# A hybrid decoder layer on one core: where the modulation columns are requested, and where four readers of small transfers stand

## The chip, the cores and the metric

One Trainium2 chip, one of its cores. The metric is the device time of one execution in microseconds (us); lower is better. TensorE is PE below (its weight loads PEld), VectorE is DVE, ScalarE is ACT, GpSimd is POOL; the SyncE queue, SP, issues the DMA transfers of this kernel.

## The reference

One layer with 256 tokens of width 2048: a SwiGLU feed-forward at half weight (FFN1), a mixer of two groups of eight heads (forgetting attention, "fox", and a gated delta rule, "gdn"), a second feed-forward (FFN2), and a final norm. Shift, scale and gate of each part come from one matrix-vector product with the condition `c`: nine vectors of 2048, that is nine times 16 columns of 128 in the kernel's layout.

```python
cond = jax.nn.silu(c)
mod = cond @ ada_w[l] + ada_b[l]
sh1, sc1, gt1, sh2, sc2, gt2, sh3, sc3, gt3 = jnp.split(mod, N_MOD, axis=-1)
h = ada_in(x, norm_g[l, 0], sh1, sc1)
x = x + MACARON_W * gt1 * swiglu(h, ffn_w_gate[l, 0], ffn_w_up[l, 0], ffn_w_down[l, 0])
h = ada_in(x, norm_g[l, 1], sh2, sc2)
x = x + gt2 * hybrid_mixer(h, w_in[l], w_out[l], ...)
h = ada_in(x, norm_g[l, 2], sh3, sc3)
x = x + MACARON_W * gt3 * swiglu(h, ffn_w_gate[l, 1], ffn_w_up[l, 1], ffn_w_down[l, 1])
return rmsnorm(x, final_norm)
```

`ada_in` is an RMS norm, scaled by 1 + scale and moved by shift. Everything is float32. In the mixer the forget gates and the delta rule's decays give one row of 256 cumulated logarithms per head and kind. The kernel needs each of these rows on all 128 partitions, and gets it there by writing the rows to DRAM and reading them back with a broadcast.

## The kernel before

**The weight stream.** All weights of the three parts are one stream of 5392 tiles of 128x128 in the order of use, read in 674 blocks of eight tiles (`Stream.next`). For each block SP fetches 512 KB (`wraw`, L125), ACT rounds it to a high part (`whi`, L128), DVE subtracts to get the low part (`wlo`, L140, called the split), and PE multiplies with both. Raw, high and low blocks have four buffers each (the raw ones five from some point on), so the cast of a block waits until PE is through with the block four before.

**Stages by block.** 0 to 111: gate and up products of the first 28 slices of FFN1, 24 matmuls to a block (L573 to L575); 112 to 167: the down projection of these (L493, L494), with a residual update per output column that is two DVE instructions (L517, L518); 168 to 231 and 232 to 263: gate/up and down of the other 16 slices; 264 to 377: the mixer's projections; 378 to 409: the output projection; 410 to 673: FFN2.

**Modulation columns.** Each of the 144 columns is a transfer of 1 MB (`adat`, L261) and a reduce on DVE that multiplies it with the condition and sums along each row (L265, which shows as two instructions, the reduce and a read of its accumulator). `ada_col` issues one transfer behind the newest weight block's transfer and records its reduce. How many are requested per block is the table `RATE`: pairs of a first block and a number of columns for each block from there on, added up in `owed`; at one, a column is requested. `ada_need` asks for those that a consumer needs and that aren't there yet. Until the mixer the reduce is recorded at once, and Tile's scheduler puts it in DVE's order where it expects its data; in the mixer and after it, it is held back until two blocks later (`settle`, `BEHIND`).

**Chains of the mixer.** While the projections run, chains of small work are advanced by a clock that counts 0.35 to a tile (`tick`): a chain is a generator that yields the time until its next part. `decays(half)` makes the decay matrix `Ln` of four heads: a subtraction from the row block (L929, on DVE) and eight exponentials (L932, on ACT). `keys(h)` prepares the keys of a head, `solve(half)` the triangular inverse of four heads, in which `U0` is read back from DRAM (L1015). `decay(h)` (L908, `dec`) and `fox(h)` (L1174, `fm`) are the start of each head's own work. The rows come by `row_of` (`rw`, L897, one head and kind) and `fetch_rows` (`x`, L921, four heads).

**What orders the work.** An engine runs its instructions in the one order that the scheduler wrote. A DVE instruction that waits for a transfer holds up every split that stands behind it. `tc.issue_after(i)` makes the scheduler place an instruction behind instruction `i`; on another engine than that of `i` it orders by time in the scheduler's plan. SP's queue is filled in the same order, so a small read stands behind the block or the column issued ahead of it.

Of the kernel before, what the change touches and what calls it, by code (L numbers as in the profile page):

```python
# [12 lines left out]
AF = mybir.ActivationFunctionType  # L13
# [3 lines left out]
P = 128  # L17
# [15 lines left out]
GR = 24  # L33
NEG = -1e30

RATE = ((0, 0.5), (28, 0.25), (33, 0.5), (49, 0.25), (56, 0.5), (66, 0.2), (112, 0.5), (168, 0.38), (264, 0.0), (284, 0.255), (376, 0.0), (424, 0.16))
N_BIG, N_GDN = 3, 3
N_FIRST = 2
AHEAD = 4
# [54 lines left out]
class Stream:  # L94
# [36 lines left out]
    def next(self, mat, k, n, width=1):  # L131
        i = len(self.order)
        if i % WB == 0:
            nc = self.nc
            b = i // WB
            r, lo = self.first.pop(0) if self.first else self.block(b)
            self.l = lo.tile([P, WB * P], F32R, name="wlo")
            pace = [r_ for r_ in RATE if r_[0] <= b][-1][1]
            with self.behind():
                lo_ = nc.vector.tensor_tensor(self.l, r, self.h.bitcast(F32), ALU.subtract)  # L140
            with self.tc.issue_after(lo_.ins):
                self.settle(b - BEHIND)
            self.owed += 0.0 if self.quiet else pace
            while self.owed >= 1.0:
                self.owed -= 1.0
                self.side()
        for d in range(width):
            self.order.append((mat, k, n, width, d))
        o = (i % WB) * P
        h, l = self.h[:, o : o + width * P], self.l[:, o : o + width * P]  # L150
        return (h, l) if width == 1 else (woven(h), woven(l))
# [3 lines left out]
def layer_kernel(ctx: ExitStack, tc: tile.TileContext, xrow, c, adaw, cols, cst, w, out, order, dbg=None):  # L155
# [600 lines left out]
    def mixer():  # L756
# [146 lines left out]
        def decay(h):  # L903

            gb = rowg.pop(h)
            gbv = gb.rearrange("p (t j) -> p t j", t=2)
            dd = m2p.tile([P, 2, P], F32, name="dec")
            V.tensor_tensor(dd, bc(C("mU")), gbv, ALU.add)  # L908
            for t in range(2):
                A.activation(dd[:, t], dd[:, t], AF.Exp, bias=ng[:, t, h : h + 1])  # L910
            A.activation(gb, gb, AF.Exp)
            return dd, gb
# [10 lines left out]
        def decays(half):  # L923

            hs4 = slice(4 * half, 4 * half + 4)
            yield 5.0
            rv = rowk[half].rearrange("p h (t j) -> p (h t) j", t=2)
            mL = C("mL").unsqueeze(1).to_broadcast([P, 8, P])
            V.tensor_tensor(Ln[:, hs4].rearrange("p h t j -> p (h t) j"), mL, rv, ALU.subtract)  # L929
            for h in range(4 * half, 4 * half + 4):  # L930
                for t in range(2):
                    A.activation(Ln[:, h, t], Ln[:, h, t], AF.Exp, bias=colS[:, t, 1, h : h + 1])  # L932
            yield 1.0
# [42 lines left out]
        def solve(half):  # L976


            hs4, n = slice(4 * half, 4 * half + 4), 2 * NH // 2
            ht = slice(n * half, n * half + n)  # L980
            V.tensor_tensor(rb2[:, :, hs4], nbeg[:, :, hs4], r2[:, :, hs4], ALU.mult)
            rk = rsqrt(ssk[:, :, hs4], [P, 2, 4], "k")
            V.tensor_tensor(rkb[:, :, hs4], rk, colS[:, :, 4, hs4], ALU.mult)
            Lh = Ln[:, hs4].rearrange("p h t j -> p (h t) j")
            yield 4.0
            for b in range(8):
                r = slice(16 * b, 16 * b + 16)
                with tc.issue_after(W.last):
                    nc.sync.dma_start(ld[ht, b].rearrange("n (r c) -> r n c", r=16), Lh[r, :, r])
                if b % 2:  # L990
                    yield 1.4
            yield 3.0
            B = slice(0, 8 * n)
            blk, xt_, pr = (x[B, j] for j in range(4, 7))
            with tc.issue_after(W.last):
                nc.sync.dma_start(blk, ld[ht].rearrange("n b e -> (n b) e"))
            yield 6.0
            G.memset(xt_, 0.0)
            G.memset(xt_[:, 0:256:17], 1.0)
            bv, xv, pv = (t_.rearrange("p (i j) -> p i j", i=16) for t_ in (blk, xt_, pr))  # L1000
            for i in range(1, 16):
                V.tensor_tensor(pv[:, :i, :i], xv[:, :i, :i], bv[:, i, :i].unsqueeze(1).to_broadcast([8 * n, i, i]), ALU.mult)
                V.tensor_reduce(xv[:, :i, i], pv[:, :i, :i], mybir.AxisListType.X, ALU.add)
                if i % 3 == 0:
                    yield 1.2
            yield 8.0
            with tc.issue_after(W.last):
                nc.sync.dma_start(lt[ht].rearrange("n b e -> (n b) e"), xt_)
            yield 3.0
            U = x[:, 7, :P].rearrange("p (n i) -> p n i", n=n)  # L1010
            with tc.issue_after(W.last):
                nc.sync.dma_start(U, lt[ht].rearrange("n b (q i) -> (b q) n i", q=16))
            yield 5.0
            for q in range(2):
                V.tensor_tensor(  # L1015
                    U0[:, hs4].rearrange("p h t (b i) -> p (h t) b i", b=4)[:, 4 * q : 4 * q + 4],
                    U[:, 4 * q : 4 * q + 4].unsqueeze(2).to_broadcast([P, 4, 4, 16]),
                    C("blk").unsqueeze(1).unsqueeze(3).to_broadcast([P, 4, 4, 16]), ALU.mult)
            if half == 0:
                fetch_rows(1)  # L1020
            yield 1.0
# [148 lines left out]
        def fox(h, qk, vt):  # L1170
            cb = rowf.pop(h)
            fm = m1p.tile([P, 384], F32, name="fm")
            for t, o, wd in ((0, 0, P), (1, P, T)):
                A.activation(fm[:, o : o + wd], cb[:, :wd], AF.Identity, bias=colS[:, t, 0, h : h + 1], scale=-1.0)  # L1174
            V.tensor_tensor(fm, fm, C("foxm"), ALU.add)
            yield 1.0
            pl = psf("plog")
            for t, o, wd in ((0, 0, P), (1, P, T)):
                sl = slice(t * P, (t + 1) * P)
                PE.matmul(pl[:, o : o + wd], qk[:, 0, sl], qk[:, 1, :wd], start=True, stop=True)  # L1180
            lg = spare(12)[:, :384]
            mx_ = tiny.tile([P, 2], F32, name="fmx")
            zz = tiny.tile([P, 2], F32, name="fzz")
            for t, o, wd in ((0, 0, P), (1, P, T)):
                V.tensor_tensor_reduce(lg[:, o : o + wd], pl[:, o : o + wd], fm[:, o : o + wd], 1.0, -3.0e38,
                                       ALU.add, ALU.max, mx_[:, t : t + 1])
            V.tensor_scalar(mx_, mx_, -1.0, None, ALU.mult)
            for t, o, wd in ((0, 0, P), (1, P, T)):
                A.activation(lg[:, o : o + wd], lg[:, o : o + wd], AF.Exp, bias=mx_[:, t : t + 1],
                             accum_out=zz[:, t : t + 1])  # L1190
            yield 3.0
            ppt = psf("ppt")
            for b in range(3):
                PE.transpose(ppt[:, b * P : (b + 1) * P], lg[:, b * P : (b + 1) * P], ident)
            pT = spare(14)[:, :384]
            A.copy(pT, ppt[:, :384])
            yield 1.0
            po = psf("pfo")
            vsl = slice((h % 4) * P, (h % 4 + 1) * P)
            PE.matmul(po[:, :P], pT[:, :P], vt[0][:, vsl], start=True, stop=True)  # L1200
            PE.matmul(po[:, P:T], pT[:, P : 2 * P], vt[0][:, vsl], start=True, stop=False)
            PE.matmul(po[:, P:T], pT[:, 2 * P :], vt[1][:, vsl], start=False, stop=True)
            ss = tiny.tile([P, 2], F32, name="fss")
            for t in range(2):
                j1 = tmp.tile([P, P], BF16, name="j1", tag="j1f")
                A.activation(j1, po[:, t * P : (t + 1) * P], AF.Square, accum_out=ss[:, t : t + 1])
            V.scalar_tensor_tensor(zz, zz, EPS, zz, ALU.mult, ALU.mult)
            V.scalar_tensor_tensor(ss, ss, 1.0 / HD, zz, ALU.mult, ALU.add)
            r = rsqrt(ss, [P, 2], "f")
            on = m1p.tile([P, 2, P], F32, name="on")  # L1210
            for t in range(2):
                V.tensor_scalar(on[:, t], po[:, t * P : (t + 1) * P], r[:, t : t + 1], None, ALU.mult)
            yield 5.0
            pf = psf("pft")
            for t in range(2):
                PE.transpose(pf[:, t * P : (t + 1) * P], on[:, t], ident)
            out_split(h, pf[:, :T], L("foxn"))
# [253 lines left out]
```

## Time and profile before

| what | value |
|---|---|
| runs | 1946.34, 1947.27, 1947.93 us; median 1947.27 |
| profiled execution | 1948.17 us, of which the span is 1946.4 us |
| granted PE clock, mean | 0.994 |
| first use of block 112 (FFN1 down) | 344.16 us |
| first use of block 168 | 495.18 us |
| first use of block 264 (mixer) | 757.0 us |
| first use of block 378 (out projection) | 1151.4 us |
| first use of block 410 (FFN2) | 1239.3 us |

Times in the profile are microseconds from the span's start. A row of the timeline is: start, duration, engine, line, operation, output and inputs, shapes, count, and in brackets how long the engine stood idle before it and what ended that. A row of waits is: engine, what waited, for what; then the sum, the number of waits and the longest, in us. A row of the table by stretches is explained where it is shown.

### The profile page before, as it was taken

How to read it: one execution, taken by the hardware profiler on the slowest of the kernel's cores; microseconds unless marked ns; L12 is line 12 of the kernel's file. 1: busy time of each engine (PE TensorE's matmuls, PEld its weight loads, DVE VectorE, ACT ScalarE, POOL GpSimd, SP SyncE). 2: the span in 40 equal slices, each digit the busy share in tenths (PEclk: the TensorE clock that was granted, in tenths of full speed). 3: DMA queues.
4: the chain of work that ended last, by engine and by line, in shares of the span. 5: the costliest groups of instructions: out<-in, count | busy, mean ns of one | idle time of the engine just before them, and what ended most of it. 6: DMA issues, size and time to landing. Idle time of an engine off the chain costs nothing.

```text
span 1946.4 us, 33719 instructions
## 1 busy us (share of the span) xinstructions
PE 1900.8 (98%) x13086; PEld 1773.9 (91%) x13087; DVE 1558.7 (80%) x2414; ACT 1040.3 (53%) x1645; POOL 56.8 (3%) x55
## 2 busy tenths in 40 slices
PE   8999998999999999999999999999999999999998
PEld 7999998888899988899989999999999999999997
DVE  6999977999999997789987988877777666666654
ACT  7444544433444445857657656665554345554553
POOL 0000000000000021000000002000000000000011
PEclk9999999999999999999999999999999999999999
DMA  9998876999998885687667557677777666666663
GB/s 383 346 359 332 309 259 241 393 386 378 353 354 352 341 333 200 219 294 244 221 232 266 171 184 238 210 264 266 263 263 267 229 201 200 204 198 202 201 201 120
DMA packets 129490, 519.58 MB, mean 267 GB/s; under 512 B 18217, under 2 KB 21545, under 8 KB 111153
## 3 DMA queue, kind: packets, MB, share of 16 engines
q1 hardware_dynamic: 129330, 517.42, 74.0%
q8 instruction: 103, 1.69, 0.3%
q14 instruction: 57, 0.47, 0.1%
HBM read 512.89 MB, written 4.47 MB: 266 GB/s over the span
## 4 chain that ended last, share of the span: by engine, by line
PE 75%; DVE 11%; DMA 5%; issue 5%; ACT 3%; SPq 0%; DVEq 0%; ACTq 0%
PE pd L493 14%; PE pg L489 10%; PE pu L489 10%; PE pd L494 7%; PE pu L490 5%; PE pg L490 5%; DVE wlo L140 4%; PE po L493 3%; DMA adat<-in_ada_dram 2%; PE pgu L575 2%; PE pgu L573 2%; PE pgu L574 2%; PE pp L796 2%; PE pp L797 2%; PE pp L798 2%
## 5 line engine op out<-in xcount | busy, mean ns | idle before, releaser
L140 DVE TENSOR_TENSOR wlo<-wraw,whi 128x1024 fp32r<-128x1024 f32 x674 | 821.0, 1225 | 256.1 <-ACT whi L128 254.8
L128 ACT CAST whi<-wraw 128x1024 fp32r<-128x1024 f32 x674 | 698.9, 1046 | 504.4 <-PE pd L493 150.9
L493 PE MATMUL pd<-hid,whi 128*128 128x512 f32 x1408 | 462.0, 382 | 0.0
L494 PE MATMUL pd<-hid,wlo 128*128 128x256 f32 x1408 | 384.7, 273 | 4.8 <-DVE wlo L140 4.8
L265 DVE CUSTOM_DVE_ANT_0 adat<-adat,cs,colt 128x2048 f32<-128x2048 f32 x142 | 334.9, 2359 | 22.6 <-DMA adat<-in_ada_dram 22.6
L489 PE MATMUL pg<-hs,whi 128*128 128x512 f32 x912 | 302.3, 382 | 0.5 <-DVE shc L440 0.5
L489 PE MATMUL pu<-hs,whi 128*128 128x512 f32 x912 | 302.1, 382 | 0.0
L493 PEld LDWEIGHTS pd<-hid,whi 128*128 128x128 f32 x1408 | 266.0, 189 | 36.8
L494 PEld LDWEIGHTS pd<-hid,wlo 128*128 128x128 f32 x1408 | 270.2, 192 | 8.2 <-DVE wlo L140 8.0
L575 PE MATMUL pgu<-hs,wlo 128*128 128x256 f32 x896 | 240.6, 278 | 14.7 <-DVE wlo L140 14.3
L490 PE MATMUL pu<-hs,wlo 128*128 128x256 f32 x912 | 249.1, 273 | 0.0
L490 PE MATMUL pg<-hs,wlo 128*128 128x256 f32 x912 | 249.1, 273 | 0.0
L573 PE MATMUL pgu<-hs,whi 128*128 128x256 f32 x896 | 244.9, 277 | 0.4 <-ACT whi L128 0.3
L574 PE MATMUL pgu<-hs,whi 128*128 128x256 f32 x896 | 244.4, 276 | 0.0
L489 PEld LDWEIGHTS pg<-hs,whi 128*128 128x128 f32 x912 | 172.4, 189 | 24.8 <-ACT shc L439 0.7
L489 PEld LDWEIGHTS pu<-hs,whi 128*128 128x128 f32 x912 | 172.4, 189 | 23.7
L796 PE MATMUL pp<-hs,whi 128*128 128x256 f32 x656 | 188.9, 289 | 1.1 <-ACT hs L380 1.1
L575 PEld LDWEIGHTS pgu<-hs,wlo 128*128 128x128 f32 x896 | 168.4, 193 | 18.4 <-DVE wlo L140 18.3
L797 PE MATMUL pp<-hs,whi 128*128 128x256 f32 x656 | 182.4, 278 | 0.0
L798 PE MATMUL pp<-hs,wlo 128*128 128x256 f32 x656 | 181.9, 277 | 0.0
L490 PEld LDWEIGHTS pu<-hs,wlo 128*128 128x128 f32 x912 | 175.0, 192 | 1.0 <-DVE wlo L140 0.9
L490 PEld LDWEIGHTS pg<-hs,wlo 128*128 128x128 f32 x912 | 175.1, 192 | 0.6
(334 smaller groups left out, 2581.4 us busy)
## 6 DMA issues: line engine op xcount, KB each, us to landing
wraw<-in_w_dram SPq DMA_DIRECT2D x674, 512.0 KB, 4.5
adat<-in_ada_dram SPq DMA_DIRECT2D x142, 1024.0 KB, 7.5
xr<-in_xr_dram SPq DMA_DIRECT2D x4, 512.0 KB, 5.4
adaf<-in_ada_dram SPq DMA_DIRECT2D x4, 512.0 KB, 8.3
xd<-x SPq DMA_DIRECT2D x4, 512.0 KB, 7.4
rw<-rowd SPq DMA_DIRECT2D x16, 128.0 KB, 4.3
x<-xd SPq DMA_DIRECT2D x4, 512.0 KB, 5.3
out_dram<-o SPq DMA_DIRECT2D x8, 256.0 KB, 2.7
```

Of the source, the lines that this page charges most:

```text
L128: self.cast = self.nc.scalar.copy(self.h, r).ins
L140: lo_ = nc.vector.tensor_tensor(self.l, r, self.h.bitcast(F32), ALU.subtract)
L265: V.tensor_tensor_reduce(t, t, cs, 1.0, L("adab", q, 1), ALU.mult, ALU.add, mod[:, q : q + 1])
L489: PE.matmul(ps, wt[0], both, start=(k == 0), stop=False)
L490: PE.matmul(ps[:, T:], wt[1], part(k, HI), start=False, stop=(k == KD - 1))
L493: PE.matmul(ps, wt[0], act.rearrange("p q (a b) -> p q b a", a=2), start=first, stop=False)
L494: PE.matmul(ps[:, :T], wt[1], woven(act[:, 0]), start=False, stop=last)
L573: PE.matmul(o, wh, part(k, HI), start=first and s == 0, stop=False, skip_group_check=skip)
L574: PE.matmul(o, wh, part(k, LO), start=False, stop=False, skip_group_check=skip)
L575: PE.matmul(o, wl, part(k, HI), start=False, stop=last, skip_group_check=skip)
L796: PE.matmul(pp[i][:, :T], wh, hh, start=(k == 0), stop=False)
L797: PE.matmul(pp[i][:, :T], wh, hl, start=False, stop=False)
```

## The change

Two things. First, `RATE`: from block 90 to block 111 no column is requested where one every five blocks was; from 168 it is 0.4 a block instead of 0.38, from 284 0.285 instead of 0.255. Requests by stage, before and now: blocks 66 to 89 4 and 4, 90 to 111 5 and 0, 112 to 167 28 and 28, 168 to 263 34 and 37, 264 to 377 24 and 26, from 410 on 17 and 17. With the requests after 112 the parity moves: 113, 115, 117 and on before, 112, 114, 116 and on now. Second, four readers of small transfers are placed behind the newest block's split (on DVE: `dec`, the subtraction for `Ln`, the two for `U0`) or cast (on ACT: `fm`), and `decays` of the second half yields 10.0 instead of 5.0 before it starts.

```diff
-RATE = ((0, 0.5), (28, 0.25), (33, 0.5), (49, 0.25), (56, 0.5), (66, 0.2), (112, 0.5), (168, 0.38), (264, 0.0), (284, 0.255), (376, 0.0), (424, 0.16))
+RATE = ((0, 0.5), (28, 0.25), (33, 0.5), (49, 0.25), (56, 0.5), (66, 0.2), (90, 0.0), (112, 0.5), (168, 0.4), (264, 0.0), (284, 0.285), (376, 0.0), (424, 0.16))
@@ Stream.next
             with self.tc.issue_after(lo_.ins):
                 self.settle(b - BEHIND)
+            self.split = lo_.ins
@@ decay(h)
-            V.tensor_tensor(dd, bc(C("mU")), gbv, ALU.add)
+            with tc.issue_after(W.split):
+                V.tensor_tensor(dd, bc(C("mU")), gbv, ALU.add)
@@ decays(half)
-            yield 5.0
+            yield 10.0 if half else 5.0
...
-            V.tensor_tensor(Ln[:, hs4].rearrange("p h t j -> p (h t) j"), mL, rv, ALU.subtract)
+            with tc.issue_after(W.split):
+                V.tensor_tensor(Ln[:, hs4].rearrange("p h t j -> p (h t) j"), mL, rv, ALU.subtract)
@@ solve(half)
-                V.tensor_tensor(
-                    U0[:, hs4].rearrange("p h t (b i) -> p (h t) b i", b=4)[:, 4 * q : 4 * q + 4],
+                with tc.issue_after(W.split):
+                    V.tensor_tensor(
+                        U0[:, hs4].rearrange("p h t (b i) -> p (h t) b i", b=4)[:, 4 * q : 4 * q + 4],
...
@@ fox(h, qk, vt)
-                A.activation(fm[:, o : o + wd], cb[:, :wd], AF.Identity, bias=colS[:, t, 0, h : h + 1], scale=-1.0)
+                with tc.issue_after(W.cast):
+                    A.activation(fm[:, o : o + wd], cb[:, :wd], AF.Identity, bias=colS[:, t, 0, h : h + 1], scale=-1.0)
```

How the order moves, at three places. The first is DVE near block 90 in the first feed-forward: `wlo` is a block's split, `adat` a column's reduce, `tg`, `tu` and `hid` finish a slice. Before:

```order
L140 TENSOR_TENSOR wlo_3488<-wraw_3484,whi_3486 128x1024
L265 ISA adat_3590,mod_124<-adat_3590,cs_86,colt_87 128x2048
L265 ISA mod_124 128x1
L591 TENSOR_TENSOR tg_3432<-pgu_3350,acc_394 128x256
L592 TENSOR_TENSOR tu_3433<-pgu_3350,acc_394 128x256
L140 TENSOR_TENSOR wlo_3528<-wraw_3524,whi_3526 128x1024
L524 TENSOR_TENSOR tu_3433<-tu_3433,tg_3432 128x256
L140 TENSOR_TENSOR wlo_3558<-wraw_3554,whi_3556 128x1024
```

The same place now:

```order
L140 TENSOR_TENSOR wlo_3485<-wraw_3481,whi_3483 128x1024
L140 TENSOR_TENSOR wlo_3525<-wraw_3521,whi_3523 128x1024
L592 TENSOR_TENSOR tg_3429<-pgu_3350,acc_394 128x256
L593 TENSOR_TENSOR tu_3430<-pgu_3350,acc_394 128x256
L525 TENSOR_TENSOR tu_3430<-tu_3430,tg_3429 128x256
L140 TENSOR_TENSOR wlo_3555<-wraw_3551,whi_3553 128x1024
```

The reduce of the column requested behind block 90, which stood three splits ahead of the split of its own block, is gone, and a split follows on a split. (Numbers of buffers and lines are off by a few between the two programs.)

The second is DVE shortly before block 112. Before, the reduce of the column requested behind block 110:

```order
L140 TENSOR_TENSOR wlo_4047<-wraw_4043,whi_4045 128x1024
L508 TENSOR_TENSOR hid_3938<-tu_3933,hid_3938 128x256
L265 ISA adat_4169,mod_124<-adat_4169,cs_86,colt_87 128x2048
L265 ISA mod_124 128x1
L591 TENSOR_TENSOR tg_3981<-pgu_3941,acc_586 128x256
L592 TENSOR_TENSOR tu_3982<-pgu_3941,acc_586 128x256
L140 TENSOR_TENSOR wlo_4087<-wraw_4083,whi_4085 128x1024
```

Now the first reduce after the pause, that of the column requested behind block 112:

```order
L140 TENSOR_TENSOR wlo_4115<-wraw_4111,whi_4113 128x1024
L525 TENSOR_TENSOR tu_3970<-tu_3970,tg_3969 128x256
L592 TENSOR_TENSOR tg_4015<-pgu_3978,acc_595 128x256
L593 TENSOR_TENSOR tu_4016<-pgu_3978,acc_595 128x256
L509 TENSOR_TENSOR hid_3975<-tu_3970,hid_3975 128x256
L266 ISA adat_4237,mod_124<-adat_4237,cs_86,colt_87 128x2048
L266 ISA mod_124 128x1
L525 TENSOR_TENSOR tu_4016<-tu_4016,tg_4015 128x256
L592 TENSOR_TENSOR tg_4061<-pgu_4024,acc_604 128x256
L593 TENSOR_TENSOR tu_4062<-pgu_4024,acc_604 128x256
L140 TENSOR_TENSOR wlo_4155<-wraw_4151,whi_4153 128x1024
```

It too stands three splits ahead of its own block's, behind the split of block 109. In the down projection behind it the fifteen pairs of residual reads (L517 and L518 before, one line further down now) stand where they stood, but for four that have one more split ahead of the pair or between its two reads, and two that have one less.

The third is ACT in the mixer, at block 284: `kk` are keys, `pk` a PSUM bank of theirs, `fm` the fox rows, `Ln` the decays. Before:

```order
L128 CAST whi_9146<-wraw_9144 128x1024
L949 ACTIVATE kk_8972<-cv_8974 128x256
L1074 ACTIVATE kbd_9974<-kk_8611,colS_8276 128x128
L1174 ACTIVATE fm_9640<-rw_9087,colS_8276 128x128
L1174 ACTIVATE fm_9640<-rw_9087,colS_8276 128x256
L945 COPY cp_9077<-pp_8981 128x256
L967 ACTIVATE j1_9065,ssk_8280<-pk_9059 128x128
L932 ACT_TABLE_LOAD
L932 ACTIVATE Ln_8284<-Ln_8284,colS_8276 128x128 x8
L967 ACTIVATE j1_9067,ssk_8280<-pk_9059 128x128
L968 COPY kk_8620<-pk_9059 128x256
```

Now:

```order
L128 CAST whi_9140<-wraw_9138 128x1024
L1078 ACTIVATE kbd_9951<-kk_8605,colS_8270 128x128
L935 ACT_TABLE_LOAD
L935 ACTIVATE Ln_8278<-Ln_8278,colS_8270 128x128 x8
L952 ACT_TABLE_LOAD
L952 ACTIVATE kk_8966<-cv_8968 128x256
L970 ACTIVATE j1_9059,ssk_8274<-pk_9053 128x128
L970 ACTIVATE j1_9061,ssk_8274<-pk_9053 128x128
L971 COPY kk_8614<-pk_9053 128x256
```

The two activations for `fm` are gone from here (they stand behind the cast of block 302 now), and the exponentials stand ahead of the keys' own activations, with a second table load behind them. SP's read for `Ln` stands behind block 285 instead of 284, with no column between. On PE the order is the same but for the keys of heads 4 to 7, which come 14 tiles later, and a few instructions that move by one to three tiles.

More of the change, by code (lines that the diff above doesn't have):

```diff
@@ L1014, in solve @@
             for q in range(2):
-                V.tensor_tensor(
-                    U0[:, hs4].rearrange("p h t (b i) -> p (h t) b i", b=4)[:, 4 * q : 4 * q + 4],
-                    U[:, 4 * q : 4 * q + 4].unsqueeze(2).to_broadcast([P, 4, 4, 16]),
-                    C("blk").unsqueeze(1).unsqueeze(3).to_broadcast([P, 4, 4, 16]), ALU.mult)
+                with tc.issue_after(W.split):
+                    V.tensor_tensor(
+                        U0[:, hs4].rearrange("p h t (b i) -> p (h t) b i", b=4)[:, 4 * q : 4 * q + 4],
+                        U[:, 4 * q : 4 * q + 4].unsqueeze(2).to_broadcast([P, 4, 4, 16]),
+                        C("blk").unsqueeze(1).unsqueeze(3).to_broadcast([P, 4, 4, 16]), ALU.mult)
             if half == 0:
```

## The prediction

> **What bounds the kernel now.** I read the page's busy shares first, then a table by stretches of the program, then the waits and the timeline of the stretch that stands out.
>
> ```profile
> span 1946.4 us, 33719 instructions
> PE 1900.8 (98%) x13086; PEld 1773.9 (91%) x13087; DVE 1558.7 (80%) x2414; ACT 1040.3 (53%) x1645; POOL 56.8 (3%) x55
> ...
> 200.00:260.00 60.00, 60.00 (x540) 60.00 (x539) 54.56 (x81) 32.10 (x45) 0.00 (x0) 1.00 0.82 300
> 265.00:345.00 80.00, 71.36 (x612) 70.25 (x611) 63.23 (x103) 37.56 (x58) 0.00 (x0) 0.98 0.67 237
> 345.00:495.00 150.00, 147.69 (x893) 134.05 (x892) 141.10 (x162) 60.13 (x60) 0.00 (x0) 1.00 0.98 386
> 495.00:660.00 165.00, 164.96 (x1003) 150.76 (x1002) 150.94 (x175) 81.34 (x122) 0.00 (x0) 1.00 0.92 354
> 830.00:1165.00 335.00, 327.38 (x2528) 311.43 (x2527) 289.05 (x710) 219.16 (x477) 0.43 (x2) 1.00 0.66 230
> ```
>
> PE is the bound: 1900.8 of 1946.4 us. What a change of order can win is the rest, 45.6 us, and the stretches (start:end, length, then PE, PEld, DVE, ACT, POOL busy with counts, PE clock, DMA share, GB/s) tell where it lies. From 200 to 260 PE never stops. From 265 to 345, the same stage with the same matmuls, it idles 80 - 71.36 = 8.64 us, though DVE and the DMA engines do less there (63.23 of 80, 0.67) than in the full stretch (54.56 of 60, 0.82). So it isn't for lack of an engine; something stands in a wrong order. At the pace of the full stretch (60 us for 540 matmuls, 0.111 us each, 24 to a block, so 2.67 us a block) the 612 matmuls need 68.0 us: the stretch has lost up to 12.0 us.
>
> ```profile
> PE pgu L575 <- DVE wlo L140: 7.1, 4, 2.8
> PE pd L494 <- DVE wlo L140: 1.5, 1, 1.5
> ...
> 259.03 1.23 DVE L140 TENSOR_TENSOR wlo<-wraw,whi 128x1024 fp32r<-128x1024 f32 x1 [0.52 <-ACT whi L128]
> 263.14 2.35 DVE L265 CUSTOM_DVE_ANT_0 adat<-adat,cs,colt 128x2048 f32<-128x2048 f32 x1 [2.88 <-DMA adat<-in_ada_dram]
> ...
> 270.72 0.43 SPq L261 DMA_DIRECT2D adat<-in_ada_dram  x1
> ...
> 273.90 1.23 DVE L140 TENSOR_TENSOR wlo<-wraw,whi 128x1024 fp32r<-128x1024 f32 x1 [0.52 <-ACT whi L128]
> 278.99 2.35 DVE L265 CUSTOM_DVE_ANT_0 adat<-adat,cs,colt 128x2048 f32<-128x2048 f32 x1 [3.87 <-DMA adat<-in_ada_dram]
> 281.94 1.22 DVE L140 TENSOR_TENSOR wlo<-wraw,whi 128x1024 fp32r<-128x1024 f32 x1
> 283.21 0.38 PE L575 MATMUL pgu<-hs,wlo 128*128 128x256 f32 x1 [1.29 <-DVE wlo L140]
> ...
> 298.94 0.38 PE L575 MATMUL pgu<-hs,wlo 128*128 128x256 f32 x1 [2.07 <-DVE wlo L140]
> 331.64 0.38 PE L575 MATMUL pgu<-hs,wlo 128*128 128x256 f32 x1 [2.78 <-DVE wlo L140]
> ```
>
> All of PE's 8.6 us (7.1 + 1.5, five waits) are for a weight split. The timeline shows why: the split at 273.90 is done at 275.1; the next instruction on DVE is the reduce of a modulation column whose 1 MB was only requested at 270.72 and is there at 279.0. DVE stands for 3.87 us, reduces for 2.35, and only then come the splits behind it: PE runs out and waits 1.29 us. Once every five blocks this repeats. The first column of the row, with 2.88 us of waiting at 263.14, costs PE nothing, so PE has a cushion of about that size, and the ones that follow eat it.
>
> **The change, part by part.** The sum is made against the profiled execution: 1948.17 us, span 1946.4 and 1.8 around it, 0.9 above the median of the runs.
>
> *Term 1, blocks 90 to 112.* Five requests (behind blocks 90, 95, 100, 105, 110) go, and with them the five reduces that stood three splits ahead of their own block. Beside the waits there is a stretch at a lower clock, straight behind the wait of 2.07 us:
>
> ```profile
> 299.00:303.00 4.00, 4.00 (x21) 4.00 (x22) 4.00 (x7) 2.77 (x4) 0.00 (x0) 0.57 0.65 190
> ```
>
> 21 matmuls in 4 us where 36 fit: 15 x 0.111 = 1.7 us lost. With the idle 8.6 that is 10.3 us at least, 12.0 at most by the matmul count above; I take 11.0. Against it stands one column requested in a bunch, behind block 112: its reduce still stands three splits ahead of its own block. It can cost nothing (the cushion is full by then, as at 263.14) or as much as the worst wait here with a slow stretch behind it, 2.78 + 1.7 = 4.5. I take nothing, since it is the first after 27 blocks without one; the ends are -12.0 and -6.5.
>
> *Term 2, the down projection after it (345 to 495).* Both versions request 28 columns there, one every other block, so the work stays; what moves is which blocks get one, and so whether a residual read stands ahead of a split.
>
> ```profile
> PE pd L494 <- DVE wlo L140: 2.3, 7, 0.6
> DVE x L517 <- PE pd L494: 8.0, 7, 2.4
> ```
>
> PE's seven waits (2.3 us, all of that stretch's idle 2.31) and DVE's seven (8.0 us, in a residual read that waits for PE's last product) are as many. In the changed order four of the fifteen pairs of reads stand a split later, so that DVE has one split more done when it waits, and two stand a split earlier; the other nine keep their place. The most to win is 2.3; the other way the waits could double, +2.3. Of eleven parts that stay or get worse against four that get better I make little: -0.5.
>
> *Term 3, the first keys of the mixer.* SP sends two small reads of DRAM behind a 1 MB column; their readers on DVE and ACT stand ahead of other work.
>
> ```profile
> 800.95 1.14 SPq L261 DMA_DIRECT2D adat<-in_ada_dram  x1
> 802.14 0.43 SPq L921 DMA_DIRECT2D x<-rowd  x1
> 802.61 1.26 SPq L897 DMA_DIRECT2D rw<-rowd  x2
> ...
> 810.34 1.22 DVE L929 TENSOR_TENSOR Ln<-cstt,x 128x1024 f32<-128x1024 f32 x1
> 812.58 0.80 ACT L1174 ACTIVATE fm<-rw,colS 128x128 f32<-128x128 f32 x2 [2.80 <-DMA rw<-rowd]
> 813.92 1.28 ACT L932 ACT_TABLE_LOAD   x1
> 815.22 2.44 ACT L932 ACTIVATE Ln<-Ln,colS 128x128 f32<-128x128 f32 x8
> 817.82 0.35 ACT L968 COPY kk<-pk 128x256 f32<-128x256 f32 x1
> 816.35 0.44 PE L961 MATMUL pk<-colt,kk 128*128 128x128 f32 x2 [1.13 <-DVE Ln L974]
> 818.22 1.22 PE L964 MATMUL pkk<-kk 128*128 128x128 f32 x4 [1.22 <-ACT kk L968]
> ...
> 818.00:822.00 4.00, 3.78 (x12) 3.27 (x13) 3.83 (x13) 3.98 (x10) 0.00 (x0) 0.57 0.12 49
> ```
>
> ACT waits 2.80 us for the fox rows; behind that on its queue stand the table load, the eight exponentials (2.44) and the copy that PE waits for: PE loses 1.13 + 1.22, and a clock of 0.57 follows, priced at 1.7 as above: 4.05 in all. The pin on the fox reader puts it some eighteen blocks later, out of this place; the exponentials keep theirs. The read for Ln goes a block later, with no 1 MB column ahead of it; on ACT one more table load (1.28) stands here. The gain lies between 0 (the Ln subtraction waits for its own read instead) and 4.05; I take -3.0, since the 2.80 us that go are more than the 2.35 that PE waits.
>
> *Term 4, the rest of the mixer.* Twenty readers are pinned in all (eight decays, eight fox rows, two Ln, two U0), each behind the newest block's split or cast.
>
> ```profile
> PE pft L1216 <- issue: 1.6, 1, 1.6
> PE po L1130 <- DVE vz L1128: 1.5, 4, 0.7
> PE pvq L1042 <- ACT qv L949: 1.0, 2, 0.6
> PE pfo L1200 <- ACT x L1196: 0.9, 2, 0.5
> ```
>
> PE idles 335 - 327.38 = 7.6 us from 830 to 1165, in small waits on chains of its own, 0.7 us at the longest of those on DVE and ACT. None of these rows names a small read, so little is to be had: at best the two waits of the first fox head (1.6 and 0.9) and a part of the rest, -4. A pinned reader comes later, and who uses its result may be late: 20 x 0.3, under half of the longest wait, is +6. What uses the results keeps its place two or more blocks behind, over 5 us at 2.67 us a block, so I take -1.0.
>
> *Term 5, the columns moved back.* Five go to later stages: three from block 168 to 263, two into the mixer. Each is one reduce of 2.35 us and one transfer. They cost nothing where DVE has room under PE: 150.94 of 165 us busy from 495 to 660, 289.05 of 335 in the mixer. Without that cover it is 5 x 2.35 = 11.8.
>
> Sum: -11.0 - 0.5 - 3.0 - 1.0 + 0 = **-15.5**: 1932.7 for the profiled execution, 1931.8 for a median, 0.8% faster.
>
> **The rivals.**
>
> *R1, the columns in a bunch take a part back.* The request behind block 112 waits like the worst now (4.5), and the down stage gets worse by 2.3 where I took 0.5 off: 1932.7 + 4.5 + 2.8 - 0.9 = 1939.1. For it: the reduce there still stands ahead of its own block. Against: the first such wait cost nothing.
>
> *R2, the pins are late, slower than before.* Behind the newest split a reader waits for a cast and thus for PE; if its chain has no slack, PE waits for each. At 0.7 us, the longest such wait, 20 readers cost 14.0; two slow stretches more 3.4, and terms 3 and 4 don't come: 1936.7 + 17.4 - 0.9 = 1953.2. It decides from 0.6 us a reader (20 x 0.6 is 12.0, and 1936.7 + 11.5 is the profiled execution). Against it: the users stand two blocks behind.
>
> *R3, the slow stretches stay.* Their 2 x 1.7 stay lost if the waits don't cause them: 1932.7 + 3.4 - 0.9 = 1935.2. For it: no such stretch follows the longest wait, 2.78 us, so waiting alone doesn't make one. Against: both lie right behind waits.
> [...]
>
> *R4, the loss only moves.* If the cover of term 5 is gone, 11.8 come back, and 2.8 from the down stage as in R1: 1932.7 + 14.6 - 0.9 = 1946.4, no change. For it: DVE is 94% busy from 345 to 495 (141.10 of 150). Against: none of the five columns goes there.
>
> **How the numbers follow.** The forecast has 0.64, R1 0.13, R3 0.07, R2 0.09, R4 0.07. 0.2% (3.9 us) is about what a measurement of this kernel can tell from no change. Faster by more are the forecast, R1 and R3, 0.84; R4 is same, 0.07; R2 slower, 0.09. The predicted time is the forecast's, 1931.8. The low end takes term 1 at -12.0, term 2 at -2.3, term 3 at -4.05 and half of term 4's best: 1948.17 - 20.4 - 0.9 = 1926.9, and 1926 in round figures; the high end holds R1, 1940. R2 and R4, 0.16, are left out.
>
> **What would show it.** Right: from 265 to 345 PE idles under 1 us and does those 612 matmuls in some 68 us; no column reduce waits for its transfer there; no stretch at 0.57 near 299. In the down stage PE's waits on the split sum to 1 to 2 us. At the first keys ACT doesn't wait for the fox rows, and PE's waits on `kk` and Ln are under 1 us. Wrong: a wait over 2 us behind the reduce of block 112's column; PE waits on `dec`, `fm`, Ln or U0's users in many heads (R2); a clock below 1 with no wait ahead of it (R3); splits late between 495 and 660, where now PE has 164.96 of 165 (R4).

## The result, and the profile after

The changed kernel takes 1939.2 us (median of 6 runs, 1937.09 to 1939.99) against 1947.6 for the kernel before beside it: a ratio of 0.9952, 95% interval 0.994 to 0.9963, or 8.4 us. 1931.8 was forecast, with a range from 1926 to 1940. The profiled execution has a span of 1937.3 us, 9.1 less than before.

First the page's first part and the table by stretches of the changed kernel (start:end, length, then PE, PEld, DVE, ACT, POOL busy with counts, PE clock, DMA share, GB/s):

```profile
span 1937.3 us, 33703 instructions
PE 1897.9 (98%) x13086; PEld 1772.2 (91%) x13087; DVE 1558.3 (80%) x2414; ACT 1038.4 (54%) x1645; POOL 55.6 (3%) x55
```

```profile
265.00:345.00 80.00, 80.00 (x683) 79.00 (x682) 66.12 (x106) 43.24 (x64) 0.00 (x0) 1.00 0.71 248
345.00:495.00 150.00, 147.90 (x895) 134.39 (x894) 140.07 (x161) 57.41 (x58) 0.00 (x0) 1.00 0.98 385
495.00:660.00 165.00, 164.89 (x997) 150.03 (x996) 152.51 (x176) 82.58 (x123) 0.00 (x0) 1.00 0.95 357
818.00:822.00 4.00, 4.00 (x21) 3.49 (x20) 3.41 (x10) 1.06 (x1) 0.00 (x0) 1.00 0.23 29
830.00:1165.00 335.00, 323.38 (x2520) 308.89 (x2519) 290.26 (x711) 219.56 (x481) 0.43 (x2) 0.99 0.65 235
```

PE no longer idles between 265 and 345 (80.00 of 80, where 71.36 stood), and no stretch at 0.57 is left near 299 or 818. But from 830 to 1165 it idles 335 - 323.38 = 11.6 us, where 7.6 stood before: the mixer got worse.

Counting PE's matmuls with the low part gives the time of each block's first use. The lead of a stage is how much earlier its first block starts than in the profile before; a term is the difference of two leads.

| from block to block | lead at the end | this stretch | forecast |
|---|---|---|---|
| 87 to 112 (end of the first gate/up) | 11.5 | -11.5 | -11.0 |
| 112 to 168 (down) | 12.1 | -0.6 | -0.5 |
| 168 to 264 (second gate/up, down) | 9.8 | +2.4 | 0 |
| 264 to 284 (first keys) | 13.8 | -4.1 | -3.0 |
| 284 to 378 (rest of the mixer) | 9.0 | +4.8 | -1.0 |
| 378 to the end | 9.1 | -0.1 | 0 |

The two losses have their rows. The waits of PE, from 655 to 740 (one row) and in the mixer (the four longest kinds):

```profile
PE pd L495 <- DVE wlo L140: 2.0, 4, 0.7
```

```profile
PE po L1134 <- DVE vz L1132: 2.5, 1, 2.5
PE ppt L1199 <- ACT x L1194: 1.5, 1, 1.5
PE po L1131 <- DVE st L1142: 1.3, 3, 0.6
PE pn L1083 <- DVE rsa_o L297: 1.2, 1, 1.2
```

In the down projection before the mixer PE waits four times for a split, 2.0 us; before it was 0.9. In the mixer one wait of 2.5 us for `vz` is new. The timeline of the changed kernel around it, SP, DVE and PE, and then the stretch behind it:

```profile
894.52 3.69 SPq L992 DMA_DIRECT2D ld<-Ln  x8
898.26 0.43 SPq L898 DMA_DIRECT2D rw<-rowd  x1
899.45 0.47 SPq L999 DMA_DIRECT2D x<-ld  x1
899.97 0.59 SPq L262 DMA_DIRECT2D adat<-in_ada_dram  x1
```

```profile
906.36 0.15 DVE L1005 TENSOR_TENSOR x<-x 64x1 f32<-64x1 f32 x1 [2.56 <-DMA x<-ld]
907.60 0.28 DVE L1132 TENSOR_TENSOR vz<-u,po 64x128 f32<-64x128 f32 x1
907.93 0.80 PE L1134 MATMUL po<-vz,At 128*128 128x128 f32 x2 [2.51 <-DVE vz L1132]
```

```profile
908.00:912.00 4.00, 4.00 (x23) 4.00 (x24) 4.00 (x5) 2.88 (x9) 0.00 (x0) 0.63 0.35 120
```

`solve(1)` writes its blocks to `ld` at 894.5 and reads them back at 899.5, just ahead of a column; the read has landed at 906.3, 6.8 us after its issue. The reader, L1005, isn't one of the four that were pinned. DVE stands 2.56 us for it, `vz` is behind it, PE idles 2.51 us and runs the next 3.4 us at a lower clock (0.50 from 907.54 to 910.95).

### The profile page after: what moved, and what is told of

Its sections match the earlier page's. It is cut to its first block, busy times and chain, and to the rows that moved or that the text cites. A ratio compares the mean times of both kernels' runs of the same rounds, so it can differ in the third digit from the quotient of the medians.

```text
span 1937.3 us, 33703 instructions
## 1 busy us (share of the span) xinstructions
PE 1897.9 (98%) x13086; PEld 1772.2 (91%) x13087; DVE 1558.3 (80%) x2414; ACT 1038.4 (54%) x1645; POOL 55.6 (3%) x55
## 4 chain that ended last, share of the span: by engine, by line
PE 77%; DVE 12%; ACT 4%; issue 3%; DMA 2%; SPq 0%; DVEq 0%; ACTq 0%
PE pd L494 13%; PE pg L490 10%; PE pu L490 10%; PE pd L495 7%; PE pu L491 5%; PE pg L491 5%; DVE wlo L140 5%; PE pgu L576 4%; PE pgu L575 4%; PE pgu L574 4%; PE po L494 3%; DVE adat L266 3%; PE pp L797 2%; PE pp L798 2%; PE pp L799 1%
## 5 line engine op out<-in xcount | busy, mean ns | idle before, releaser
L576 PEld LDWEIGHTS pgu<-hs,wlo 128*128 128x128 f32 x896 | 167.8, 192 | 10.5 <-DVE wlo L140 10.4
```

The lines of the kernel that those rows point to most:

```text
L576: PE.matmul(o, wl, part(k, HI), start=False, stop=last, skip_group_check=skip)
```

## The experiments

All are compared with the kernel before on the same chip, in at least five executions each; ratios have their 95% intervals, and a gain in us is worked out from the ratio where nothing else is said. The profiled executions differ by up to 2.5 us before block 20, and by up to 1.6 in the wait at 106, behind which some have a slow stretch of the clock and some have none (the pause alone 0.90 from 100 to 108 and 0.89 from 108 to 116, the kernel before and the changed kernel 1.00 in both); so leads are counted from block 87.

**The pause alone.**

```diff
-... (66, 0.2), (112, 0.5), (168, 0.38), (264, 0.0), (284, 0.255), ...
+... (66, 0.2), (90, 0.0), (112, 0.5), (168, 0.38), (264, 0.0), (284, 0.255), ...
```

> The kernel before with one edit of the table: no columns from block 90 to 111, every later rate as before (0.38 and 0.255), no pins. Theory (the five columns of that stretch cost 11.5 us by their place, and what they do later costs little): block 112 starts 11.5 us earlier, PE has no wait on a split from 265 to 333, the time is about 1947.4 - 11.5 - 0.6 = 1935. Rival (the columns have to be read at some time, and their price comes back further on, where they are forced together): block 112 starts 11.5 us earlier too, but the time is 1943 or more.

Ratio 0.9978 (0.9969 to 0.9988): 4.3 us, the rival. Block 112 leads by 11.5 us, and blocks 168 to 264 lose nothing (12.1 and 12.1). But the lead falls to 8.4 at block 378 and to 4.5 at block 410: the five columns that nobody asked for earlier are forced behind blocks 401 to 409, where the next part needs them. The waits of PE from 1142 to 1245, the output projection:

```profile
PE po L494 <- DVE wlo L140: 2.1, 3, 0.8
PE pg L434 <- DVE wlo L140: 0.8, 1, 0.8
```

In the changed kernel no wait for a split stands there. So about 4 us of the pause's gain hang on the higher rates later.

**The old columns, in another place on DVE.** For the nine columns requested behind blocks 66 to 111, the reduce is held behind the split of its own block; all columns stay where they are requested.

```diff
+            self.split, self.at = lo_.ins, b
...
-            with nullcontext() if W.late else W.behind(False):
+            here = 66 <= len(W.order) // WB < 112
+            with nullcontext() if W.late else tc.issue_after(W.split) if here else W.behind(False):
```

> The kernel before with all its columns at their old blocks, but from block 66 to 111 each reduce is placed behind the split of its own block, not up to three splits ahead of it. Theory (the place of the reduce on DVE is at fault, not its 2.35 us or its 1 MB): PE's waits between 265 and 345 go, block 112 starts 10 us or more earlier, the time is about 1937. Rival (the 1 MB transfer or the 2.35 us of DVE is what PE waits for): the waits stay, the time stays at 1947.

Ratio 0.995 (0.9937 to 0.9962): 9.8 us, as much as the whole change. (Its profile is of the longest of its six runs, 1943.37 against a median of 1939.42, and has a lead of 6.6 at the end.) Block 112 leads by 11.5 us, as with the pause. The stretch, PE's one wait in it, and one of the reduces:

```profile
265.00:345.00 80.00, 79.42 (x683) 78.35 (x682) 72.30 (x112) 43.64 (x66) 0.00 (x0) 1.00 0.81 283
```

```profile
PE pd L496 <- DVE wlo L140: 0.6, 1, 0.6
```

```profile
281.80 1.23 DVE L140 TENSOR_TENSOR wlo<-wraw,whi 128x1024 fp32r<-128x1024 f32 x1 [0.82 <-ACT whi L128]
282.94 2.35 DVE L267 CUSTOM_DVE_ANT_0 adat<-adat,cs,colt 128x2048 f32<-128x2048 f32 x1
```

PE does the same 683 matmuls as in the changed kernel, with DVE at 72.3 us instead of 66.1 and the DMA share at 0.81 instead of 0.71. The reduce no longer waits: its data is there when its own block's split is done. So in this stretch the column's 2.35 us and its 1 MB weren't the trouble.

**The pins alone**, with the later second half of the decays and the old table.

> The changed kernel with the old table of rates: the four pins and the later second half of the decays alone. Theory (pins win 4 us at the first keys, and pins with the later second half lose 4 to 5 us between blocks 300 and 340, where DVE now waits for a read of ld): block 112 starts as before, block 284 is 4 us ahead of before, block 340 about level, the time is 1947 within 1.5. Rival (the loss between 300 and 340 comes from the more frequent columns of the new table): block 340 stays 4 us ahead and the time is 1943 to 1944.

Ratio 0.9982 (0.9972 to 0.9991): 3.5 us, the rival's time; the lead at block 340 lies between the two. Leads: 4.8 at block 284, of which 1.1 are from before block 112 and 3.7 from the first keys; 2.6 at block 340, 3.8 at block 378. The first keys came out as said; the loss behind them is 2.1 up to block 340 and 1.0 up to 378, not 4 to 5. So the loss in the changed kernel isn't the pins' alone.

**The new table alone**, no pins, and both halves of the decays at 5.0.

> The kernel before with the whole new table of rates and no pins. Theory (the pause saves 11.5 us, and the higher later rates are what keeps the five columns from being forced in the output projection, where the pause alone lost 4 us): block 410 stays at the lead of block 378, the time is 8 us below before; with the pins, worth 3.5 alone, the two then overlap. Rival (the higher rates win nothing against the pause alone): 4 to 5 us below before.

Ratio 0.9951 (0.9939 to 0.9963): 9.6 us, all that the whole change has. As said, block 410 stays at the lead of block 378 (9.0 and 9.1). At the first keys it wins 2.1 us, about half of the changed kernel's 4.1, though a wait for the key copy remains. The pause alone wins 1.7 there, with neither a pin nor the new rate of the mixer. Neither profile has the slow stretch that stood near 818 before (0.50 from 818.22 to 821.63), priced at 1.7 in the prediction: the granted clock is 1.00 from 807 to 819 in both, and in the version without the pin on `fm`. From 284 to 378 it loses 2.8. PE's row at the keys and DVE's wait for `ld`:

```profile
809.26 0.60 PE L964 MATMUL pkk<-kk 128*128 128x128 f32 x3 [1.95 <-ACT kk L968]
```

```profile
DVE x L1002 <- DMA x<-ld: 5.3, 1, 5.3
```

This is the first half's read, sent at 825.6 with a column 0.6 us behind it. The pause alone has the same wait, 4.4 us, at the old rate of the mixer, so a late read of `ld` needs neither pins nor denser columns. The second half's read, the one that costs the changed kernel its 2.5 us, is in time here and in the pins alone: DVE doesn't wait for it in either. It is late only where the later half and the new table meet.

**The second half of the decays at 5.0 again**, all else as changed.

```diff
-            yield 10.0 if half else 5.0
+            yield 5.0
```

> The changed kernel with the second half of the decays yielding 5.0 as before, not 10.0. Theory (the later second half is what brings the read of ld behind a column and in front of vz): the wait of 2.5 us at vz near 908 goes, the time is 2 to 4 us below the changed kernel, 12 us below before. Rival (the half that comes earlier meets other readers): the wait goes and others come between blocks 300 and 320, the time is that of the changed kernel, 9 us below before, or more.

Ratio 0.9937 (0.9925 to 0.9949): 12.3 us, the theory. In the profile the lead is 13.9 at block 284 and 13.7 at block 378: of 4.8 us of loss 0.2 is left. The mixer's stretch, and SP and DVE at the read:

```profile
830.00:1165.00 335.00, 327.48 (x2548) 311.97 (x2547) 294.14 (x719) 222.13 (x486) 0.55 (x3) 1.00 0.67 239
```

```profile
894.30 0.48 SPq L999 DMA_DIRECT2D x<-ld  x1
...
897.05 0.42 SPq L262 DMA_DIRECT2D adat<-in_ada_dram  x1
```

```profile
899.59 0.15 DVE L1005 TENSOR_TENSOR x<-x 64x1 f32<-64x1 f32 x1
```

The read goes 2.75 us ahead of the next column instead of 0.5, is there when its reader starts, 5.3 us after the issue (in the changed kernel it takes 6.8), and DVE doesn't wait for it at all. In the changed kernel a column is sent 0.52 us behind this read and DVE waits 2.6 us for it; it waits 2.3 us in that kernel's second profile and 2.9 without the pin on `fm`. The interval overlaps that of the changed kernel (0.994 to 0.9963) by a little; the profile's 4.6 us tell them apart.

**A fifth pin**, on the reader of `ld`.

```diff
-                V.tensor_tensor(pv[:, :i, :i], xv[:, :i, :i], ...)
+                with nullcontext() if i > 1 else tc.issue_after(W.split):
+                    V.tensor_tensor(pv[:, :i, :i], xv[:, :i, :i], ...)
```

> The changed kernel with a fifth reader pinned: the first DVE instruction that reads the 16x16 blocks back from ld stands behind the newest split too. Theory (at 905 DVE stands 2.6 us for that read with vz behind it, PE idles 2.5 us for vz and runs 3.4 us at half clock, which costs another 1.7): both go, the time is 1939.2 - 4.2 = 1935. Rival (the wait goes on to the next link of that chain, U0 or the heads' own solves come late): the wait at vz goes, others of its size come between blocks 320 and 360, the time is 1938 to 1941.

Ratio 0.9946 (0.9934 to 0.9958): 10.5 us, between the two numbers, and by the runs not clear of the changed kernel. DVE's rows:

```profile
908.48 0.28 DVE L1133 TENSOR_TENSOR vz<-u,po 64x128 f32<-64x128 f32 x1
...
916.06 0.14 DVE L1006 TENSOR_TENSOR x<-x 64x1 f32<-64x1 f32 x1
```

`vz` now runs ahead of the reader, which waits for nothing, and PE's wait is gone. The lead at block 320 is 12.6 (9.4 in the changed kernel), at the end 12.1 (9.1): 3.0 us in the profile. No later link of the chain took a wait of that size over: the longest wait of PE behind it is 1.1 us.

**Without the pin on `fm`.**

```diff
-                with tc.issue_after(W.cast):
+                if True:
                     A.activation(fm[:, o : o + wd], ...)
```

> The changed kernel without the pin on fm (ACT); the pins on dec, Ln and U0 stay. Theory (at block 284 the fox reader on ACT held up the exponentials and the key copy, 4 us with the slow stretch): the wait of ACT for the fox rows near 812 comes back, PE waits 1 to 2 us at the first keys, block 300 loses 3 to 4 us of its lead, the time is 6 to 7 us below before. Rival (the later half of the decays and the pin on Ln made that gain): block 300 keeps its lead, the time stays at 9 us below before.

Ratio 0.9962 (0.995 to 0.9974): 7.4 us, not clear of the changed kernel by the runs. In the profile ACT waits 1.0 us for the fox rows again, PE 1.4 for the key copy where 0.3 stood, and the first keys win 3.0 instead of 4.1 us. The pin on `fm` is worth about 1 us there, not the 3 to 4 that the theory gave it; of the rest, 1.7 to 2.1 us come without any pin, as the pause and the table alone show.

**0.38 from block 168**, with the missing columns in the mixer (0.318) and the decays at 5.0.

> The changed kernel with the second half of the decays at 5.0, 0.38 instead of 0.4 from block 168, and 0.318 instead of 0.285 from 284, so that the columns still are there in time. Theory (0.4 is what lost 2.4 us between blocks 168 and 264, the later half of the decays what lost 4 to 5 between 300 and 340): blocks 168 to 264 lose nothing, 13 to 15 us below before. Rival (the three columns that now go into the mixer cost there what they cost before it): blocks 168 to 264 lose nothing, the mixer loses 2 to 3 more, 11 to 12 us below before.

Ratio 0.9955 (0.9942 to 0.9967): 8.8 us, the rival's side, and less than its 11 to 12. Blocks 168 to 264 lose nothing (12.1 and 12.1), so it is the 0.4 that costs 2.4 us; whether by the number of columns or by the blocks that they fall on wasn't tried. The mixer loses 5.7 from block 284 on:

```profile
PE pd L495 <- DVE wlo L140: 0.6, 1, 0.6
```

```profile
858.56 0.38 PE L797 MATMUL pp<-hs,whi 128*128 128x256 f32 x1 [2.29 <-ACT whi L128]
```

One wait is left between 655 and 740 (first row), and the mixer has a new one of 2.29 us for a cast.

**All columns at their old rates, placed, with the pins.** The old table, reduces behind their own blocks' splits from block 66 to the mixer, the pin on `ld`, the second half of the decays at 10.0.

> The changed kernel with the old table of rates, each reduce from block 66 to the mixer placed behind the split of its own block, and the reader of ld pinned. Theory (place is what counts, and the gains add up: 9.8 us of the place alone, 3.5 of the pins alone, 2 to 3 of the ld reader): 13 to 16 us below before. Rival (the later columns of the old table leave a wait in the feed-forward behind the mixer and in its middle): 10 to 12 us below before.

Ratio 0.9936 (0.9924 to 0.9949): 12.5 us, between the two. The lead is 13.5 us at block 498 and 11.1 at block 542. DVE and PE at the start of FFN2's first down projection:

```profile
1466.84 2.35 DVE L267 CUSTOM_DVE_ANT_0 adat<-adat,cs,colt 128x2048 f32<-128x2048 f32 x1 [2.71 <-DMA adat<-in_ada_dram]
...
1472.06 0.42 DVE L510 TENSOR_TENSOR hid<-tu,hid 128x256 fp32r<-128x256 f32 x1
```

```profile
1472.53 0.48 PE L495 MATMUL pd<-hid,whi 128*128 128x512 f32 x1 [2.30 <-DVE hid L510]
```

It is the trouble of blocks 90 to 112 again: the column requested behind block 503 stands three splits ahead of its own block, and `hid` behind it. The same wait, of 2.0 and 1.4 us, is in the profiles of the placed reduces alone and of the pins alone, which have the old table too. The kernel before has the same order and DVE waits only 0.21 us there; why the column comes later in the three wasn't tried.

**The same with 0.2 a block from 424**, so that nothing is requested behind 503.

> The version with the old table, reduces behind their own blocks' splits and the ld reader pinned, with one number more changed: 0.2 instead of 0.16 columns a block from block 424, so that no column is requested behind blocks 503 and 509. Theory (there DVE stood 2.4 to 2.7 us for such a column with the second feed-forward's hid behind it, and PE idled 2.3 us at the start of the last down projection): that wait goes, block 542 keeps the lead of block 498, 13.5 us in the profile, the time is 13 to 15 us below before. Rival (the more frequent columns make another stretch of that stage late): the lead at block 630 is 11 us again.

Ratio 0.9942 (0.9928 to 0.9956), 11.1 us by the medians, 1936.2 (1935.74 to 1939.49). The wait is gone and the lead of block 498, 13.0, is kept to the end (13.1), as the theory has it. The time is short of the 13 to 15 us expected, and by the runs it isn't told apart from the one above.

**A version put together, and the changed kernel again on its chip.** The pins, the placed reduces, both halves of the decays at 5.0, 0.5 from block 111, 0.38 from 168, 0.285 from 284, 0.16 from 429.

> A version put together from the runs so far: the pins with both halves of the decays at 5.0; from block 66 to the mixer each reduce behind the split of its own block, so no pause at 90 but requests at even blocks from 112; 0.38 from 168, 0.285 from 284, 0.16 from 429. Theory (each part keeps what it won alone): 11.5 to 12 us at block 168, no loss from 168 to 264 as with 0.38 before, 3 to 4 at the first keys, nothing lost later: 14 to 16 us below before, 5 to 7 below the changed kernel. Rival (the gains overlap in the mixer): 12 us below before, as with the second half at 5.0 alone.

> The changed kernel once more, on the chip of the version put together: 9 us below before, as in its first comparison (ratio 0.9952); it is what the two others of this call are compared with.

The version takes 1937.89 us (1937.09 to 1938.52), ratio 0.9945 (0.9932 to 0.9957); the changed kernel 1941.49 (1940.70 to 1942.13), 0.9963 (0.995 to 0.9977). On one chip the runs don't overlap: 3.6 us less than the changed kernel, under the 5 to 7 expected; 10.7 below before is also under the rival's 12. It loses 1.8 us from block 112 to 168, where the changed kernel wins 0.6; PE waits there for two splits, 0.96 and 0.45 us, that it doesn't wait for in the changed kernel. The changed kernel's second profile has the same leads as its first, within 0.3 us at each stage and 9.1 at the end.

## Why the prediction was right, and what was mis-sized

The time lies in the range, and the sign and the first two terms came as worked out. That it lies in the range is in part luck: 1939.2 is 7.4 us above the forecast, and the range reached up to 1940 for R1, which didn't happen. The mechanism of term 1 is shown from both sides: take the columns away, or leave them and move only their reduces, and block 112 starts 11.5 us earlier in either case. The column requested behind block 112 cost nothing, as taken. The changed kernel's reduces between 265 and 345 waited 0.2 us in all, and PE has no wait there:

```profile
L266 DVE CUSTOM_DVE_ANT_0 adat<-adat,cs,colt 128x2048 f32<-128x2048 f32 x3 | 7.0, 2339 | 0.2 <-DMA adat<-in_ada_dram 0.2
```

Term 2 was -0.6 against -0.5. Term 3 was -4.1 against -3.0, the full 4.05 that the rows bounded; its cause was told too narrowly, since the pin on `fm` holds only about 1 us of it, and about half came without any pin.

The step that was mis-sized is term 4: "None of these rows names a small read, so little is to be had", with -1.0 and an upper end of +6 for the pinned readers. It cost +4.8, inside the bounds, but not by the pinned readers being late. The rows of before have no wait of PE on a small read in the mixer, but DVE did wait for such reads there, without a wait of PE of that size behind it:

```profile
DVE dec L908 <- DMA rw<-rowd: 2.7, 1, 2.7
DVE U L1015 <- DMA x<-lt: 2.1, 1, 2.1
```

So PE's rows alone didn't tell what a DVE wait of this size would cost with `vz` behind it. The change moved `solve(1)` by the 14 tiles of the later half, and with the new table its read of `ld` left 0.5 us ahead of a 1 MB column. An unpinned reader became the wait. The later half at 5.0 takes 4.6 of the 4.8 back, the fifth pin 3.0.

Term 5 was taken at nothing, for DVE's 14 us of room from 495 to 660; it cost 2.4 (0.4 against 0.38, shown by the version that goes back to 0.38). The stretch that was read for the cover is the gate/up stage, and it loses 0.7 us by the leads, with no wait long enough to name. The other 1.6 are lost in the down projection behind it, where residual reads and columns stand together: two more waits for a split, 2.0 us against 0.9.

R1 gave 1939.1, what was measured, but not by its mechanism: neither the column behind block 112 nor the down stage behind it took anything back. R2 fell: PE has no such wait in many heads. R4 fell for this table, but the pause alone shows how near it was: there the lead shrinks by 5.4 us in the mixer (by which of its waits wasn't tried) and by 3.9 in the output projection, where columns are forced. R3's question is below.

## What to carry to other kernels

In this kernel a wait on a transfer held up what stood behind it on the engine's queue (at 278.99 in the kernel before DVE waits 3.87 us for a column, and PE then 1.29 us for the split behind it), so first ask whether the waiting instruction can stand later, before the transfer is moved or dropped: placing nine reduces behind their own blocks' splits won as much as the whole change. A table of rates is a sum that has to come out: what is left out in one stage is forced in another, and the price there has to be read from that other stage's own rows, down projection and gate/up apart. Whoever moves a chain in time moves its transfers past other transfers (the read of `ld` took 6.8 us with a column 0.52 us behind it, and no more than 5.3 with one 2.75 us behind it); list every reader of DRAM on that chain, pinned or not.

## What was not expected of the hardware

In these profiles the lower clock behind a wait of PE comes or doesn't, at one length of the wait. In the kernel before the wait of 2.07 us had a slow stretch (0.50 from 299.40 to 302.81) and that of 2.78 had none (1.00 from 330.11 to 336.93). The pins alone have waits in the first feed-forward of 2.10 us, with full speed behind it (1.00 from 286 to 290), and of 2.70 us, with a slow stretch (0.64 from 333 to 337). The changed kernel's second profile has a wait of 2.25 us for `vz` and full speed behind it (1.00 from 910 to 914), where the first had a slow stretch behind 2.51 (0.50 from 907.54 to 910.95). So here the length alone doesn't decide.

What goes with it is where the wait falls. In the profiles of the kernel before and of the changed kernel each slow stretch is 3.41 us long or twice that (753.37 to 760.20 and 743.70 to 750.53, but for the one that the end cuts off), and within a profile they all begin on one raster of 3.41 us: in the kernel before, 299.40 and 818.22 are 152 steps apart, in the changed kernel 743.70 and 907.54 are 48. The rows cut the time on that raster. First the kernel before, around its two longest waits (they end at 298.94 and 331.64), then the two profiles of the changed kernel around `vz`:

```profile
295.98:299.40 3.42, 1.35 (x12) 1.16 (x12) 3.42 (x7) 0.56 (x2) 0.00 (x0) 1.00 0.08 31
299.40:302.81 3.41, 3.41 (x19) 3.41 (x18) 3.40 (x6) 2.63 (x4) 0.00 (x0) 0.50 0.71 205
326.70:330.11 3.41, 2.16 (x20) 1.97 (x18) 2.68 (x4) 0.00 (x0) 0.00 (x0) 1.00 0.26 99
330.11:333.52 3.41, 1.88 (x16) 1.88 (x17) 3.41 (x8) 1.98 (x4) 0.00 (x0) 1.00 0.27 64
```

```profile
904.13:907.54 3.41, 1.29 (x12) 1.10 (x10) 1.18 (x12) 2.12 (x6) 0.00 (x0) 1.00 0.87 346
907.54:910.95 3.41, 3.02 (x14) 3.02 (x15) 3.35 (x7) 2.15 (x8) 0.00 (x0) 0.50 0.16 42
```

```profile
905.25:908.66 3.41, 2.44 (x22) 2.25 (x21) 1.03 (x8) 3.26 (x8) 0.00 (x0) 1.00 1.01 403
908.66:912.08 3.42, 2.14 (x19) 2.14 (x20) 3.36 (x16) 1.57 (x7) 0.00 (x0) 1.00 0.13 54
```

The wait of 2.07 us lies in one step of the raster and leaves PE 1.35 us of work there; the next step runs at 0.50. The wait of 2.78 us is cut in two by the raster, the two steps keep 2.16 and 1.88 us, and the clock stays at 1.00. It is the same for 2.51 us (1.29 left, 0.50 in the next step) and 2.25 us (2.44 and 2.14 left, 1.00 behind). In the profiles of the kernel before and of the changed kernel, from 20 us on, all seven steps at full clock with 1.35 us of PE or less have a slow one behind them, and none of those with 1.64 or more has. So R3's premise doesn't hold for these stretches: each stands behind idle time of PE, and in these profiles one came or didn't with how that time fell on the raster.

In these two profiles of the changed kernel the slow stretch isn't simply added to the wait. The second has none at `vz` (1.00 from 910 to 914) and loses 4.6 us from block 300 to 320 all the same, where the first (0.50 from 907.54 to 910.95) loses 4.4; PE idles 7.2 us there instead of 5.9.
